# Neighbourhood attention: the value sums of two neighbouring units share one PSUM bank and are copied and added together

## The chip, the cores and the metric

One core of a Trainium2 chip. The kernel is one launch that computes a whole encoder layer for two sequences. The time is the device time of the launch in microseconds (us); three runs of the kernel before gave 2685.11, 2685.29 and 2685.42, median 2685.29. Engines: PE is TensorE's matmul row and PEld its weight loads, DVE is VectorE, ACT is ScalarE, POOL is GpSimd, SP is SyncE (it only issues DMAs).

## The reference

A layer runs two token mixers beside each other on the same input projection: 2-D neighbourhood attention and a bidirectional mLSTM. Both are gated, projected, merged and projected out. The change lies in the attention over the grid tokens (64 columns wide, 16 and 32 rows). Per row of queries and block of 16 columns it is:

```python
s_win = jnp.einsum('bcqhd,bwckhd->bhcqwk', q_blk, k_blk).astype(jnp.float32) * scale
s_win = jnp.where(valid[:, :, None, :], s_win + bias, NEG)
s_met = jnp.einsum('bcqhd,bmhd->bhcqm', q_blk, km).astype(jnp.float32) * scale
p = jax.nn.softmax(jnp.concatenate([s_met, s_win], axis=-1), axis=-1).astype(v.dtype)
return (jnp.einsum('bhcqm,bmhd->bcqhd', p_met, vm)
        + jnp.einsum('bhcqwk,bwckhd->bcqhd', p_win, v_blk))
```

A query sees 8 rows and 16 columns of keys around it and 16 learned meta tokens. The result is multiplied by silu(z) before the projection.

## The kernel before

All products run in single precision by splitting operands into a high and a low part (three matmuls, lines L218 to L220, for most dense products). TensorE's order is written by hand; the instructions of the other engines are ordered by a scheduler that simulates the program while it is built, and that also chooses which buffer of a pool a new tile gets.

The program has a sparse chain (mLSTM and attention, for the two sequences in turn) and a dense chain (input projections L787 to L789 and L988 to L990, final projections L1949 to L1951). A generator yields costs from the sparse chain, and dense matmuls are put between its steps until they have made up the cost. So in an attention stage TensorE always has dense matmuls between two steps of attention, and attention's other work runs on DVE and ACT meanwhile.

Attention walks over units. A unit is one tile of 8 query rows, one head of 64 channels and one block of 16 columns, 128 queries in all; the four blocks of a head follow each other. There are 64 units in the first stage and 128 in the second, 192 in all. A unit goes through a pipeline, spread over four to five rounds u of a loop with four steps each:

- round u: the scores (two matmuls L1236 and L1237, a "score group") go into a bank with the tag "sc" (one bank) for even units and "sm" (two banks) for odd ones; DVE adds the bias and finds the maximum (L1240); ACT takes the exponential (L1251, out of the bank to the tile prb)
- round u + 1: DVE divides by the sum (L1260, L1261)
- round u + 2: TensorE transposes the probabilities (L1268), ACT takes the high part (L1270) and DVE the low part (L1275)
- round u + 3, last step: three or four matmuls L1283 (a "value group") multiply by the values. The stationary operand holds the values' high part for output rows 0 to 63 and the low part for rows 64 to 127; the moving one holds the probabilities' high part in columns 0 to 127 and the low part in columns 128 to 255. So one "sm" bank gets four products in its first 256 columns, of which three are needed
- round u + 4: ACT copies one of them to the output tile yg (L1291, first step of the round), and DVE adds the two others in place (L1298, after the scaling in the round's second step), 64 partitions by 128 columns each. With the last block of a pair of heads yg is multiplied by the gate (L1300) and stored.

So an "sm" bank is taken three times in two rounds: by two value groups, which each keep it until their adds are done, and by one score group, which keeps it until its exponential is done.

Of the kernel before, what the change touches and what calls it, by code (L numbers as in the profile page):

```python
# [13 lines left out]
AF = mybir.ActivationFunctionType  # L14
ALU = mybir.AluOpType
# [3 lines left out]
P = 128  # L19
# [56 lines left out]
def _row_types(R):  # L76

    out = []
    for t in range(R // 8):
        if t == 0:  # L80
            out.append((0, 0, 11))
        elif t == R // 8 - 1:
            out.append((2, R - 12, 12))
        else:
            out.append((1, 8 * t - 4, 15))
    return out
# [52 lines left out]
class K:  # L139
# [964 lines left out]
    def na(self, s, rts):  # L1104

        tc, nc, i = self.tc, self.nc, self.i
        rows = _row_types(SEQLEN[s] // 64)
        with tc.tile_pool(name=f"na{s}{rts[0]}", bufs=1, side="right", reuse_waits="tile") as np_:
            self.qB = [np_.tile([P, 4, P], F32R, name=f"qB{j}") for j in range(2)]
            self.kx = [np_.tile([P, 16, 64], F32R, name=f"kx{j}") for j in range(2)]  # L1110
            self.gts = [np_.tile([P, 17, 48], F32, name=f"gt{j}") for j in range(2)]
            for q in self.qB:
                nc.gpsimd.dma_start(q[64:128], i["onehot"].rearrange("a (b c) -> a b c", b=4))
            for g in self.gts:
                nc.gpsimd.memset(g[:, 0, :], 0.0)
                nc.gpsimd.memset(g[:, 16, :], 0.0)
            heads = [(rt, pr, hh) for rt in rts for pr in range(4) for hh in range(2)]
            n = len(heads)
            prep = self.na_prep(np_, s, rows, heads, 0)
            self.na_bias(rows, heads, 0)  # L1120
            for k in range(6):
                next(prep, None)
                for _ in range(2 if k else 17 - 5 * s):
                    yield A_N[s]
            cur, nxt = self.head, None
            units = [(j, cb) for j in range(n) for cb in range(4)]
            ready = {}
            n_ = len(units)
            for u in range(n_ + 4):
                if u >= 4:  # L1130
                    self.na_copy(ready[u - 4])
                if u < n_:
                    j, cb = units[u]
                    if cb == 0:
                        cur = self.head
                        prep = self.na_prep(np_, s, rows, heads, j + 1) if j + 1 < n else iter(())
                        next(prep, None)
                    ready[u] = [cur, heads[j], cb, None, None, self.gts[j % 2], None]
                    self.na_scores(np_, ready[u], rows)
                    if j + 1 < n and cb == 0:  # L1140
                        self.na_bias(rows, heads, j + 1)
                yield A_N[s]
                if u < n_:
                    self.na_exp(np_, ready[u])
                if 1 <= u <= n_:
                    self.na_scale(np_, ready[u - 1])
                if u >= 4:
                    self.na_add(ready.pop(u - 4), s)
                if u < n_ and cb:
                    next(prep, None)  # L1150
                if u == n_ + 3:
                    break
                yield A_N[s]
                if 2 <= u <= n_ + 1:
                    self.na_turn(np_, ready[u - 2])
                    if u < n_ and cb >= 2:
                        next(prep, None)
                yield A_N[s]
                if 2 <= u <= n_ + 1:
                    self.na_low(ready[u - 2])  # L1160
                if u >= 3:
                    self.na_out(ready[u - 3])
                yield A_N[s]

    def na_bias(self, rows, heads, j):
# [108 lines left out]
        pts, pt, (_, _, nb, ks) = unit[4], unit[6], unit[3]  # L1274
        self.nc.vector.tensor_tensor(pts[:ks, :nb, 1, :], pt[:ks, :nb], pts[:ks, :nb, 0, :].bitcast(F32), op=ALU.subtract)  # L1275

    def na_out(self, unit):
        nc = self.nc
        vt, cb, (_, _, nb, ks), pts = unit[0][3], unit[2], unit[3], unit[4]
        kc = KC0[cb]  # L1280
        av = self.psum("sm", [P, 512])
        for ch in range(nb):
            nc.tensor.matmul(av[:, :256], vt[:ks, kc // 8 + ch].rearrange("p a b -> p (a b)"),  # L1283
                             pts[:ks, ch].rearrange("p a b -> p (a b)"), start=ch == 0, stop=ch == nb - 1)
        unit[6] = av

    def na_copy(self, unit):
        yg, cb, av, h0 = unit[0][4], unit[2], unit[6], unit[1][2] * 64
        yv = yg.rearrange("p (r b c) -> p b r c", r=8, b=4)[h0:h0 + 64, cb]
        rc = lambda x: x.rearrange("p (r c) -> p r c", r=8)  # L1290
        self.nc.scalar.activation(yv, rc(av[64:128, 0:P]), AF.Copy)  # L1291
        unit[4] = yv, rc

    def na_add(self, unit, s):
        nc = self.nc
        (_, _, _, _, yg, zt), (rt, pr, hh), cb, _, (yv, rc), _, av = unit
        for c in (0, P):
            nc.vector.tensor_tensor(yv, rc(av[0:64, c:c + P]), yv, op=ALU.add)  # L1298
        if hh and cb == 3:
            nc.vector.tensor_tensor(yg, yg, zt, op=ALU.mult)  # L1300
            nc.sync.dma_start(self.YA[s][rt][pr][:, :], yg)
            self.done.add(("na", s, rt, pr))
# [900 lines left out]
```

## Time and profile before

| | |
|---|---|
| median of 3 runs | 2685.29 us |
| profiled execution | 2684.88 us |
| its span, first to last instruction | 2682.8 us |
| mean granted TensorE clock | 0.996 |
| PE, PEld busy | 2640.1, 2330.7 us |
| DVE, ACT, POOL busy | 1940.1, 1441.0, 195.3 us |

The profile is of one execution. A row of a group of instructions gives the line, the engine, the operation, the tile written and the tiles read, the shapes and the count; behind the bar the busy time in us and the mean duration of one in ns; behind the second bar the idle time of the engine just before these instructions and what ended it. A row of the list of waits gives who waited for whom, the total in us, how many times, and the longest. A row of the timeline gives the start, the duration, the engine and the instruction, and in brackets how long the engine was idle before it. A row by stretches gives the stretch, its width, the busy time and count of PE, PEld, DVE, ACT and POOL, the granted clock, the share of the DMA engines and GB/s. A matmul's end is modelled, since matmuls overlap.

### The profile page before, as it was taken

The page shows a single profiled execution, that of the slowest core. Times are in us where ns is not written, and L with a number is a line of the kernel's source. Part 1 is how long each engine was busy: PE and PEld are TensorE (multiplying, and loading weights), DVE is VectorE, ACT ScalarE, POOL GpSimd, SP SyncE. Part 2 cuts the span into 40 slices and gives each one's busy share as a digit, 9 for nine tenths or more (in the row PEclk, how much of TensorE's full clock was granted, in tenths as well). Part 3 has the DMA queues.
Part 4 walks back from the last instruction along what each step waited for, and adds up shares of the span by engine and source line. Part 5 has one row for each costly group of instructions (what it writes and reads, how often), then busy time and mean ns, then how long its engine had stood idle before and what let it go on. Part 6 is the DMA issues. An engine that isn't in the chain of part 4 may idle for free.

```text
span 2682.8 us, 47074 instructions
## 1 busy us (share of the span) xinstructions
PE 2640.1 (98%) x15928; PEld 2330.7 (87%) x15928; DVE 1940.1 (72%) x5262; ACT 1441.0 (54%) x3388; POOL 195.3 (7%) x418
## 2 busy tenths in 40 slices
PE   9999998999999999999999999999999999999998
PEld 7998897899978999888888888887889898989888
DVE  5655678788667878546686776867478989898954
ACT  5423555554445655546665666656366666656521
POOL 0111130011301115000000000000000000000000
PEclk9999999999999999999999999999999999999999
DMA  9899988799866998978889998899899999998975
GB/s 370 331 334 335 331 289 306 278 339 312 294 223 235 328 331 289 319 234 285 261 270 346 362 299 261 273 351 336 281 312 319 288 306 287 280 304 261 310 255 209
DMA packets 393520, 800.49 MB, mean 298 GB/s; under 512 B 50528, under 2 KB 173360, under 8 KB 389440
## 3 DMA queue, kind: packets, MB, share of 16 engines
q1 hardware_dynamic: 361728, 697.24, 77.9%
q0 software_dynamic: 31552, 100.25, 10.1%
q8 instruction: 126, 2.06, 0.3%
q14 instruction: 114, 0.93, 0.1%
HBM read 543.72 MB, written 253.60 MB: 297 GB/s over the span
## 4 chain that ended last, share of the span: by engine, by line
PE 89%; DVE 4%; DMA 4%; ACT 1%; issue 1%; SPq 0%; POOL 0%; DVEq 0%; ACTq 0%
PE pj L218 9%; PE pj L220 9%; PE pj L219 9%; PE pj L988 8%; PE pj L990 7%; PE pj L989 7%; PE pj L787 5%; PE pj L789 5%; PE pj L788 5%; PE pj L1950 3%; PE pj L1949 3%; PE pj L1951 3%; PE sm L1283 3%; PE tr L1268 2%; DMA whl<-w 1%
## 5 line engine op out<-in xcount | busy, mean ns | idle before, releaser
L218 PE MATMUL pj<-xh,whl 128*128 128x512 f32 (+1 forms) x960 | 369.5, 385 | 8.2 <-DMA whl<-w 6.2
L220 PE MATMUL pj<-xh,whl 128*128 128x512 f32 (+1 forms) x960 | 361.3, 376 | 0.0
L219 PE MATMUL pj<-xl,whl 128*128 128x512 f32 (+1 forms) x960 | 360.4, 375 | 0.2 <-DVE xl L446 0.2
L787 PE MATMUL pj<-whl,xh 128*128 128x256 f32 (+1 forms) x1152 | 330.7, 287 | 0.0
L789 PE MATMUL pj<-whl,xl 128*128 128x256 f32 (+1 forms) x1152 | 327.0, 284 | 0.0
L788 PE MATMUL pj<-whl,xh 128*128 128x256 f32 (+1 forms) x1152 | 326.7, 284 | 0.0
L787 PEld LDWEIGHTS pj<-whl,xh 128*128 128x128 f32 x1152 | 219.0, 190 | 0.4
L1949 PE MATMUL pj<-whl,mh 128*128 128x256 f32 x768 | 218.3, 284 | 0.9 <-DMA whl<-w 0.9
L788 PEld LDWEIGHTS pj<-whl,xh 128*128 128x128 f32 x1152 | 218.9, 190 | 0.2
L789 PEld LDWEIGHTS pj<-whl,xl 128*128 128x128 f32 x1152 | 218.8, 190 | 0.0
L218 PEld LDWEIGHTS pj<-xh,whl 128*128 128x128 f32 x960 | 181.2, 189 | 40.8 <-issue 5.3
L1950 PE MATMUL pj<-whl,mh 128*128 128x256 f32 x768 | 216.3, 282 | 0.0
L1951 PE MATMUL pj<-whl,mlo 128*128 128x256 f32 x768 | 215.5, 281 | 0.0
L220 PEld LDWEIGHTS pj<-xh,whl 128*128 128x128 f32 x960 | 181.3, 189 | 35.0
L219 PEld LDWEIGHTS pj<-xl,whl 128*128 128x128 f32 x960 | 181.6, 189 | 30.4 <-issue 1.0
L988 PE MATMUL pj<-xh,whl 128*128 128x512 f32 x512 | 206.7, 404 | 1.1 <-ACT pj L1005 1.1
L990 PE MATMUL pj<-xh,whl 128*128 128x512 f32 x512 | 202.0, 395 | 0.0
L989 PE MATMUL pj<-xl,whl 128*128 128x512 f32 x512 | 201.0, 393 | 0.0
L1275 DVE TENSOR_TENSOR pts<-tr,pts 96x384 fp32r<-96x384 f32 (+2 forms) x192 | 118.6, 617 | 57.2 <-ACT pts L1270 55.2
L1270 ACT ACTIVATE pts<-tr 96x384 fp32r<-96x384 f32 (+2 forms) x192 | 103.6, 539 | 100.8 <-PE tr L1268 100.1
L218 PE MATMUL pj<-yh,whl 128*128 128x512 f32 x384 | 154.1, 401 | 0.0
L219 PE MATMUL pj<-yl,whl 128*128 128x512 f32 x384 | 151.5, 394 | 0.7 <-DVE yl L1851 0.7
(380 smaller groups left out, 6866.1 us busy)
## 6 DMA issues: line engine op xcount, KB each, us to landing
whl<-w SPq DMA_DIRECT2D x131, 1024.0 KB
whl<-q SPq DMA_DIRECT2D x112, 512.0 KB
w<-whl SPq DMA_DIRECT2D x36, 1024.0 KB
wraw<-wu SPq DMA_DIRECT2D x48, 512.0 KB
gt<-st SPq DMA_DIRECT2D x96, 256.0 KB
tg<-gt SPq DMA_DIRECT2D x96, 256.0 KB
q<-po POOLq DMA_DIRECT2D x26, 512.0 KB, 6.7
xt<-xt SPq DMA_DIRECT2D x24, 512.0 KB
```

Source lines behind the costliest of these rows:

```text
L218: mm(out, ah, bh, start=start, stop=False)
L219: mm(out, ah, bl, start=False, stop=False)
L220: mm(out, al, bh, start=False, stop=stop)
L787: nc.tensor.matmul(o, xh, wh, start=k == 0, stop=False)
L788: nc.tensor.matmul(o, xh, wl, start=False, stop=False)
L789: nc.tensor.matmul(o, xl, wh, start=False, stop=k == KT - 1)
L988: mm(bank, w[:, 0, k], xh[:, k], start=fresh and k == 0, stop=False, skip_group_check=True)
L989: mm(bank, w[:, 0, k], xl[:, k], start=False, stop=False, skip_group_check=True)
L990: mm(bank, w[:, 1, k], xh[:, k], start=False, stop=k == 3, skip_group_check=True)
L1949: nc.tensor.matmul(o, mh[:, k, xs], wh, start=clear > 0 and k == 0, stop=False)
L1950: nc.tensor.matmul(o, mh[:, k, xs], wl, start=False, stop=False)
L1951: nc.tensor.matmul(o, ml[:, k, xs], wh, start=False, stop=clear < 2 and k == KT - 1)
```

## The change

A bank "sm" is taken for two neighbouring units. The value group of the even unit writes columns 0 to 255 and that of the odd unit, one round later, columns 256 to 511. When the odd one is done, one copy and two adds handle both units: they work on 64 partitions by 2 x 128 columns. They stand where the odd unit's stood: the copy in the first step of the next round, the adds in its second step (behind the last unit, directly after the copy). Copies go from 192 to 96 and adds from 384 to 192. Matmuls keep their number, their shapes and their order.

```diff
             for u in range(n_ + 4):
-                if u >= 4:
-                    self.na_copy(ready[u - 4])
+                if u >= 5 and u % 2:
+                    self.na_copy(ready[u - 5], pairs[u - 5])
+                    if u > n_:
+                        self.na_add(ready[u - 5], pairs.pop(u - 5), s)
...
-                if u >= 4:
-                    self.na_add(ready.pop(u - 4), s)
+                if 5 <= u <= n_ and u % 2:
+                    self.na_add(ready[u - 5], pairs.pop(u - 5), s)
...
                 if u >= 3:
-                    self.na_out(ready[u - 3])
+                    if u % 2:
+                        pairs[u - 3] = self.psum("sm", [P, 512])
+                    self.na_out(ready[u - 3], pairs[(u - 3) // 2 * 2])
...
-    def na_out(self, unit):
+    def na_out(self, unit, av):
...
-        av = self.psum("sm", [P, 512])
+        o = av[:, cb % 2 * 256:cb % 2 * 256 + 256]
         for ch in range(nb):
-            nc.tensor.matmul(av[:, :256], vt[:ks, kc // 8 + ch].rearrange("p a b -> p (a b)"),
+            nc.tensor.matmul(o, vt[:ks, kc // 8 + ch].rearrange("p a b -> p (a b)"),
...
+    def na_copy(self, unit, av):
+        h0 = unit[1][2] * 64
+        yv = unit[0][4].rearrange("p (r b c) -> p b r c", r=8, b=4)[h0:h0 + 64, unit[2]:unit[2] + 2]
+        rc = lambda x: x.rearrange("p (b q r c) -> p b q r c", b=2, q=2, r=8)
+        self.nc.scalar.activation(yv, rc(av[64:128])[:, :, 0], AF.Copy)
...
-        for c in (0, P):
-            nc.vector.tensor_tensor(yv, rc(av[0:64, c:c + P]), yv, op=ALU.add)
-        if hh and cb == 3:
+        for q in range(2):
+            nc.vector.tensor_tensor(yv, rc(av[0:64])[:, :, q], yv, op=ALU.add)
+        if hh and cb == 2:
```

Lines behind the change stand 5 lower in the changed file up to the value group (score group L1241 and L1242, transposes L1273, value group L1288), the copy is L1295, the adds are L1302 and the gate L1304.

What a group of matmuls on an "sm" bank waits for, counted in the two built programs by the last instruction of DVE and ACT that its first matmul names:

| | before | changed |
|---|---|---|
| score groups on "sm" | 96: 92 an add, 4 nothing of DVE or ACT | 96: 3 an add, 5 an exponential, 88 nothing of DVE or ACT |
| value groups that take a bank | 192: 58 an add, 42 an exponential, 92 only their own low part | 96: 42 an add, 50 an exponential, 4 only their own low part |
| value groups on the second half | none | 96: only their own low part |

TensorE at the place of the program that runs at 889 to 893 us in the profile before. The dense matmuls are those on "pj"; the names in brackets are the semaphores that an instruction waits for, DVE_49 that of VectorE, Activation_49 that of ScalarE, PE_49 TensorE's own, DMAHW those of DMAs. Before:

```order
L218 MATMUL pj<-xh,whl 128x512
L219 MATMUL pj<-xl,whl 128x512
L220 MATMUL pj<-xh,whl 128x512
L1283 MATMUL sm<-pts,vt 128x256 [waits DVE_49]
L1283 MATMUL sm<-pts,vt 128x256 x2
L1236 MATMUL sm<-kd,stk 128x288 [waits DVE_49,Activation_49]
```

And changed:

```order
L218 MATMUL pj<-xh,whl 128x512
L219 MATMUL pj<-xl,whl 128x512
L220 MATMUL pj<-xh,whl 128x512
L1288 MATMUL sm<-pts,vt 128x256 [waits DVE_49]
L1288 MATMUL sm<-pts,vt 128x256 x2
L1241 MATMUL sm<-kd,stk 128x288 [waits PE_49]
```

No matmul has moved; the score group no longer names VectorE and ScalarE.

VectorE at the same place. "xr" is a tile of other work (it prepares weights for later), "yg" is written by the adds, L1240 and L1245 are the bias and maximum. Before:

```order
L641 TENSOR_TENSOR xr<-xh,xl 128x1024 x2
L1298 TENSOR_TENSOR yg<-sm,yg 64x8x16
L1260 RECIPROCAL sm<-sm 128x1
L1275 TENSOR_TENSOR pts<-tr,pts 96x3x128
L1212 TENSOR_TENSOR kx_9711<-kx_9711,kd 64x768
L1298 TENSOR_TENSOR yg<-sm,yg 64x8x16
L1261 TENSOR_SCALAR prb<-prb,sm 128x384
L705 SCALAR_TENSOR_TENSOR st<-st 128x512
L1298 TENSOR_TENSOR yg<-sm,yg 64x8x16
L1240 ISA sm,mx<-sm,gt_9712 128x288
```

And changed:

```order
L641 TENSOR_TENSOR xr<-xh,xl 128x1024 x2
L1265 RECIPROCAL sm<-sm 128x1
L1280 TENSOR_TENSOR pts<-tr,pts 96x3x128
L1217 TENSOR_TENSOR kx_9711<-kx_9711,kd 64x768
L1266 TENSOR_SCALAR prb<-prb,sm 128x384
L1245 ISA sm,mx<-sm,gt_9712 128x288
L1245 ISA mx 128x1
L705 SCALAR_TENSOR_TENSOR st<-st 128x512
L641 TENSOR_TENSOR xr<-xr 128x512
L1302 TENSOR_TENSOR yg<-sm,yg 64x2x8x16
```

The two adds of the even unit, which stood ahead of the score's maximum, are gone; the pair's first add stands behind it. Elsewhere the scheduler has also moved rows that the change does not touch: in 210 places on DVE, 88 on ACT, 12 on POOL and 56 on SP, nearly all of them by a few rows.

More of the change, by code (lines that the diff above doesn't have):

```diff
@@ L1128, in na @@
             n_ = len(units)
+            pairs = {}
             for u in range(n_ + 4):
-                if u >= 4:
-                    self.na_copy(ready[u - 4])
+                if u >= 5 and u % 2:
+                    self.na_copy(ready[u - 5], pairs[u - 5])
+                    if u > n_:
+                        self.na_add(ready[u - 5], pairs.pop(u - 5), s)
                 if u < n_:
@@ L1280, in na_out, with na_add @@
         kc = KC0[cb]
-        av = self.psum("sm", [P, 512])
+        o = av[:, cb % 2 * 256:cb % 2 * 256 + 256]
         for ch in range(nb):
-            nc.tensor.matmul(av[:, :256], vt[:ks, kc // 8 + ch].rearrange("p a b -> p (a b)"),
+            nc.tensor.matmul(o, vt[:ks, kc // 8 + ch].rearrange("p a b -> p (a b)"),
                              pts[:ks, ch].rearrange("p a b -> p (a b)"), start=ch == 0, stop=ch == nb - 1)
[L1285 to L1291, printed above, removed]
+    def na_copy(self, unit, av):
[3 more added lines that the diff above has]
+        self.nc.scalar.activation(yv, rc(av[64:128])[:, :, 0], AF.Copy)
         unit[4] = yv, rc
-    def na_add(self, unit, s):
+    def na_add(self, unit, av, s):
         nc = self.nc
-        (_, _, _, _, yg, zt), (rt, pr, hh), cb, _, (yv, rc), _, av = unit
-        for c in (0, P):
-            nc.vector.tensor_tensor(yv, rc(av[0:64, c:c + P]), yv, op=ALU.add)
-        if hh and cb == 3:
+        (_, _, _, _, yg, zt), (rt, pr, hh), cb, _, (yv, rc) = unit[:5]
+        for q in range(2):
+            nc.vector.tensor_tensor(yv, rc(av[0:64])[:, :, q], yv, op=ALU.add)
+        if hh and cb == 2:
             nc.vector.tensor_tensor(yg, yg, zt, op=ALU.mult)
```

## The prediction

> **What bounds the kernel now.** I read the page's totals and its chain first, then the two stages in which the changed code runs (their first and last instructions of lines L1291 and L1298 lie at 851.8 and 2575.6 us), then the waits of TensorE, and last the place of the longest wait. The totals and the chain:
>
> ```profile
> span 2682.8 us, 47074 instructions
> ...
> PE 2640.1 (98%) x15928; PEld 2330.7 (87%) x15928; DVE 1940.1 (72%) x5262; ACT 1441.0 (54%) x3388; POOL 195.3 (7%) x418
> ...
> PE 89%; DVE 4%; DMA 4%; ACT 1%; issue 1%; SPq 0%; POOL 0%; DVEq 0%; ACTq 0%
> ```
>
> TensorE's matmul row (PE) is busy for 2640.1 of 2682.8 us and makes up 89% of the chain. VectorE (DVE) and ScalarE (ACT), on which the change removes work, have 28% and 46% to spare. So what the change does to the time is what it does to TensorE's waits. The two attention stages, from the table by stretches (width, then busy time of each engine, granted clock, DMA share, GB/s):
>
> ```profile
> 853.00:1072.00 219.00, 215.61 (x1645) 208.38 (x1644) 178.02 (x426) 123.40 (x253) 60.96 (x109) 0.99 0.89 304
> 1987.00:2577.00 590.00, 585.20 (x3898) 533.37 (x3899) 514.87 (x1299) 354.10 (x854) 2.31 (x4) 1.00 0.93 293
> ```
>
> PE is idle there for 3.4 + 4.8 = 8.2 us in all. TensorE's list of waits says for whom (total us, times, longest):
>
> ```profile
> PE pj L218 <- DMA whl<-w: 6.2, 2, 3.9
> PE sm L1236 <- DVE yg L1298: 4.3, 5, 1.9
> ...
> PE sm L1283 <- ACT prb L1251: 2.0, 3, 1.3
> ...
> PE sm L1236 <- DVE sm L1260: 1.5, 2, 0.9
> ...
> PE sm L1283 <- DVE yg L1298: 0.2, 1, 0.2
> ```
>
> The last four are all that attention's own matmuls wait for, and all are waits for one of the two "sm" banks: the score group L1236 for 4.3 + 1.5 us, the value group L1283 for 2.0 + 0.2. (L1260 is the instruction that ended nearest; the score group itself names only an add and a copy.) The longest of them in order of time:
>
> ```profile
> 889.60 0.52 PE L1283 MATMUL sm<-pts,vt 96*128 96x256 f32 x3
> ...
> 889.78 0.28 DVE L1298 TENSOR_TENSOR yg<-sm,yg 64x128 f32<-64x128 f32 x1
> ...
> 890.10 0.16 DVE L1260 RECIPROCAL sm<-sm 128x1 f32<-128x1 f32 x1
> 890.18 0.53 DVE L1275 TENSOR_TENSOR pts<-tr,pts 96x384 fp32r<-96x384 f32 x1
> ...
> 890.63 0.94 DVE L1212 TENSOR_TENSOR kx<-kx,kd 64x768 fp32r<-64x768 f32 x1
> ...
> 891.60 0.28 DVE L1298 TENSOR_TENSOR yg<-sm,yg 64x128 f32<-64x128 f32 x1
> ...
> 892.03 0.37 PE L1236 MATMUL sm<-kd,stk 128*128 128x288 f32 x1 [1.91 <-DVE yg L1298]
> ...
> 892.37 0.28 PE L787 MATMUL pj<-whl,xh 128*128 128x264 f32 x1
> ...
> 892.49 0.28 PE L788 MATMUL pj<-whl,xh 128*128 128x264 f32 x1
> ...
> 893.14 0.42 PE L789 MATMUL pj<-whl,xl 128*128 128x264 f32 x1
> ...
> 893.36 0.42 PE L787 MATMUL pj<-whl,xh 128*128 128x264 f32 x1
> ```
>
> The two adds of one unit do not follow each other on VectorE: three other operations stand between them, the second ends at 891.88, and only then may the score group write. Two things are read off beside it. Matmuls in a row start 0.12 us apart and last 0.28, so a wait costs its idle time and 0.16 more. And from 893.14 on they start 0.22 apart. The table by stretches of 3.4 us around it:
>
> ```profile
> 889.35:892.76 3.41, 1.50 (x11) 1.25 (x10) 3.28 (x8) 3.31 (x6) 0.00 (x0) 1.00 1.04 396
> 892.76:896.18 3.42, 3.42 (x18) 3.42 (x17) 3.27 (x10) 0.59 (x2) 0.00 (x0) 0.50 1.05 393
> 896.18:899.60 3.42, 3.42 (x31) 3.42 (x30) 3.05 (x7) 0.87 (x2) 0.00 (x0) 1.00 0.99 342
> ```
>
> After a stretch in which PE worked for 1.50 of 3.41 us the granted clock is 0.50 for 3.42 us, with 18 matmuls instead of 31.
>
> **The change part by part.** *Removed work.* The rows by line, of the changed operations and of two that move 256 columns from a bank as the new ones do:
>
> ```profile
> L1298 DVE TENSOR_TENSOR yg<-sm,yg 64x128 f32<-64x128 f32 x384 | 107.7, 281 | 27.6 <-ACT yg L1291 20.6
> ...
> L1291 ACT ACTIVATE yg<-sm 64x128 f32<-64x128 f32 x192 | 52.6, 274 | 67.0 <-PE sm L1283 63.5
> L1956 DVE TENSOR_TENSOR yo<-pj,gain 128x256 f32<-128x256 f32 x96 | 40.4, 421 | 42.4 <-ACT sqj L1955 41.8
> L1955 ACT ACTIVATE sqj<-pj 128x256 bf16<-128x256 f32 x96 | 36.6, 381 | 64.3 <-PE pj L1951 56.1 <-DVE yo L1956 7.6
> ```
>
> 384 adds of 281 ns (107.7 us) become 192, which I price at the 421 ns of L1956: 80.8 us, 26.9 less on VectorE. 192 copies of 274 ns (52.6 us) become 96 at the 381 ns of L1955: 36.6 us, 16.0 less on ScalarE. Both lie beside TensorE's work, which covers them: 0 on the path. If that cover went, at most the 42.9 us would count.
>
> *Score groups.* (The counts here and below are of waits in the two built programs, given with the change.) Of the 96 that use an "sm" bank, 92 name an add before; 3 do in the changed program, and 5 an exponential of two rounds ago. Of the 7 waits that go, the cost is 4.3 + 1.5 + 7 x 0.16 = 6.9 us. I take -6.9; nothing is late next for them, since a matmul of the same stream stands ahead.
>
> *Clock.* If the 1.91 us at 892.03 go, PE has no hole there, and the stretch of half clock with it. At 0.22 instead of 0.12 us a matmul, 3.42 us did the work of 1.87: -1.6 (-1.7 by the clock's 0.50, -1.4 by 18 matmuls against 31).
>
> *Value groups, exponential.* A pair's bank is taken in every second round, and which of the two it is was settled by the scheduler. 42 of 192 value groups name the exponential before and 50 of 96 now. Their price today is 2.0 + 3 x 0.16 = 2.5 us; by 50/42 it becomes 3.0: +0.5.
>
> *Value groups, adds.* 58 of 192 name an add before, at 0.2 + 0.16 = 0.4 us in all; now 42 do, the other first groups of pairs. For each the copy and adds end later: 0.38 + 2 x 0.42 against 0.27 + 2 x 0.28, 0.39 us more. This wait is not in the trace. Its low bound is the present rate of value groups, 42/58 x 0.4, a change of -0.1. Its high bound is the rate of the score groups, 6.9/92 a piece: 42 x 0.075 = 3.2, a change of +2.8. I take +1.8, two thirds up, because the chain is longer and TensorE is not asked for less in between. Behind such a wait stands all of TensorE: the next dense matmuls.
>
> *Order of the rest.* Rows of DVE, ACT, SP and POOL that the change does not touch stand in a few hundred other places from about 893 us on; TensorE's do not. I price it at 0. A weight load that comes late is the row to bound it with: 3.9 + 0.16, so +4.1; a wait of that kind that goes is worth about as much the other way in principle, but attention has none.
>
> Sum: -6.9 - 1.6 + 0.5 + 1.8 = -6.2 us. The profiled execution took 2684.88 us (the span and 2.1 around it), so 2678.7; the median of the runs is 0.4 above it, so 2679.1, 0.23% less.
>
> **Rivals.** *The wait moves over (no change).* The pair's first group takes up all that the score groups leave: 6.9 for the adds in place of 1.8, -6.9 - 1.6 + 0.5 + 6.9, about 2684.2. For it: the same adds on the same crowded VectorE, 0.39 us later, and value groups that already wait for an exponential. Against it: the value group comes three quarters of a round behind the score group, and in 58 cases such a group waited once.
>
> *The clock stretch stays (no change).* Then the sum lacks 1.6: 2680.7. For it: only one stretch is concerned, and a hole of another origin can bring it back. Against it: the table's three rows. [...]
>
> *A late weight load (no change).* The order of SP's queue moves in 56 places, among them four loads "whl<-w". One late by 4.1 us gives 2683.2. Against it: in attention no such wait stands in the list.
>
> *The freed engines reach the end (faster).* If the shorter queues of VectorE and ScalarE also clear the value groups' waits, all of them go: -6.9 - 1.6 - 2.5 - 0.4 = -11.4, 2673.9. [...]
>
> *The longer hold is in the way (slower).* A pair's bank is held for two rounds and freed 0.39 us later. Where TensorE reaches the next pair before that, each of 96 pairs costs 0.39. To be 0.2% slower, the 8.5 us gained, less 0.5, and 5.4 more have to be eaten: 13.4 / 0.39 = 34 pairs. With 40 of them 2692.8. For it: VectorE is busy 178.0 of 219.0 us in the first stage and 514.9 of 590.0 in the second. Against it: 7 waits in 92 score groups, which come sooner after the adds.
>
> **How the numbers follow.** 0.2% is 5.4 us, about what a measurement of this kernel can tell from no change: 2679.9 and 2690.7 are the bounds. The forecast has 0.42 and is faster; the engines freed 0.09, faster; the wait that moves 0.20, the clock 0.10, the late load 0.08, all within; the longer hold 0.11, slower. That makes 0.51 faster, 0.38 within and 0.11 slower. The forecast alone spans 2677.2 to 2680.1 by the bounds of its adds. The range for 8 in 10 goes from the 2673.9 of the freed engines to 2687, where the late load is added to a wait that has moved over (2684.2 + 4.1, less part of the clock) and the longer hold begins.
>
> **What would show it.** Right: no idle of PE at the score groups for an add, a list in which value groups wait for the adds by 1 to 3 us and for the exponential by about 3, a clock of 1.00 at 893 to 896 us, 192 adds near 421 ns and 96 copies near 381. Wrong: adds or copies much longer than that; waits of the value groups near 9 us; a wait for "whl" in attention; a new stretch of half clock.

## The result, and the profile after

The changed kernel took 2677.35 us (median of 7 runs, 2675.68 to 2681.7); the kernel before, run beside it, 2685.11 (7 runs, 2681.5 to 2686.68). The ratio is 0.9977 with a 95% interval of 0.9967 to 0.9986, so it is faster by 0.23%. In a second session it was 2679.09 against 2684.69, ratio 0.9979 (0.9970 to 0.9988). One of that session's 11 runs of the changed kernel took 4314.22 us at a granted clock of 0.556, as one of the third session's 15 of the kernel before took 3208.49 at 0.751; the ratios leave both out. The forecast of 2679.1 equals the second of the two medians, and both medians are inside the likeliest case's own range (2677.2 to 2680.1). The total was right; two of its terms and a term set to zero were off, and partly cancelled.

The totals and the chain of the changed kernel's page:

```profile
span 2673.9 us, 46686 instructions
...
PE 2637.4 (99%) x15928; PEld 2329.0 (87%) x15928; DVE 1916.3 (72%) x5070; ACT 1424.9 (53%) x3292; POOL 195.7 (7%) x418
...
PE 87%; DMA 7%; DVE 4%; ACT 2%; issue 1%; SPq 0%; DVEq 0%; ACTq 0%
```

The span is 8.9 us shorter, while DVE is busy 23.8 us less and ACT 16.1 less: the saved work did not come off the time one for one. The rows by line of what was merged, and of the two groups that share the "sm" banks:

```profile
L1288 PE MATMUL sm<-pts,vt 96*128 96x256 f32 (+2 forms) x672 | 116.1, 289 | 5.0 <-ACT prb L1256 4.1 <-DVE yg L1302 0.7
...
L1302 DVE TENSOR_TENSOR yg<-sm,yg 64x256 f32<-64x256 f32 x192 | 79.6, 414 | 15.5 <-ACT yg L1295 12.1
...
L1295 ACT ACTIVATE yg<-sm 64x256 f32<-64x256 f32 x96 | 36.6, 381 | 31.9 <-PE sm L1288 26.3 <-DMA zt<-nz 1.3 <-DMA kx<-nk 1.3
...
L1241 PE MATMUL sm<-kd,stk 128*128 128x384 f32 (+2 forms) x96 | 32.6, 340 | 0.0
```

An add of both units takes 414 ns and a copy 381, against the 421 and 381 that the forecast took from L1956 and L1955. The score groups on "sm" (L1241 now) have no idle time left. Of TensorE's list of waits, the rows that answer to those of before:

```profile
PE sm L1288 <- ACT prb L1256: 4.1, 6, 1.4
PE pj L218 <- DMA whl<-w: 3.4, 1, 3.4
...
PE sm L1347 <- issue: 2.0, 1, 2.0
...
PE sm L1288 <- DVE yg L1302: 0.7, 1, 0.7
```

The value groups' wait for an exponential has doubled (2.0 to 4.1). At L1347, a gate matmul of the second mLSTM stage, there is a wait that was 0.5 us before (L1343); "issue" means that the profile found nothing that released it.

To see where the time went I cut the program at the same four matmuls in every kernel: the first score group of attention's stage one, the last matmul of its last value group, the first score group of stage two, and the last value group's last matmul. All kernels here issue the same 15928 matmuls in the same order, so the stretches can be compared. Between the cuts, the table by stretches of the kernel before (width, busy time of PE, PEld, DVE, ACT and POOL, clock, DMA share, GB/s; rows: stage one, middle, stage two):

```profile
833.93:1196.71 362.78, 359.11 (x2365) 328.26 (x2363) 257.87 (x629) 197.44 (x410) 63.84 (x124) 1.00 0.88 295
1196.71:1936.16 739.45, 734.80 (x3655) 611.44 (x3654) 509.35 (x1702) 441.55 (x1162) 4.11 (x22) 1.00 0.91 301
1936.16:2573.26 637.10, 632.10 (x4122) 571.82 (x4121) 543.60 (x1374) 385.81 (x924) 2.31 (x4) 1.00 0.93 294
```

And of the changed kernel:

```profile
828.40:1185.29 356.89, 356.61 (x2365) 326.46 (x2364) 249.12 (x565) 191.53 (x378) 64.22 (x124) 1.00 0.87 300
1185.29:1927.21 741.92, 735.50 (x3655) 611.42 (x3654) 509.15 (x1702) 442.33 (x1162) 4.10 (x22) 1.00 0.90 300
1927.21:2564.32 637.11, 632.15 (x4122) 572.30 (x4121) 528.28 (x1246) 374.06 (x860) 2.18 (x4) 1.00 0.93 294
```

Stage one is 5.9 us shorter: PE's idle time there went from 3.7 us (362.78 - 359.11) to 0.3, and PE's busy time fell by the 2.5 that matmuls at half clock (1.5, at 892 us) and behind waits had taken. Stage two is as long as before, with 5.0 us idle in both. The middle, which the change does not touch, is 2.5 us longer. The rest of the span's difference, 5.5 us, lies ahead of attention (833.93 against 828.40), where every engine issues the same instructions in the same order in both programs: over the 13 profiles of this study that first part took between 828.4 and 836.4 us. TensorE's waits there for a late weight load (L218 for "whl<-w") are 6.2 us in the profile before and 3.4 in this one; half clock lasts for 10.2 us there in both. So of the 8.9 us between these two profiles 5.5 are put down to chance, and 3.4 belong to attention and the middle (4.6 between the second profiles of the two kernels). The medians, with the scatter of the first part in them, say 7.8 and 5.6; the 1 to 4 us by which they are larger are found in no stretch here.

### The profile page after: what moved, and what is told of

Same layout as the page of the kernel before. It is cut to its first block, busy times and chain, and to the rows that moved or that the text cites. A ratio compares the mean times of both kernels' runs of the same rounds, so it can differ in the third digit from the quotient of the medians.

```text
span 2673.9 us, 46686 instructions
## 1 busy us (share of the span) xinstructions
PE 2637.4 (99%) x15928; PEld 2329.0 (87%) x15928; DVE 1916.3 (72%) x5070; ACT 1424.9 (53%) x3292; POOL 195.7 (7%) x418
## 4 chain that ended last, share of the span: by engine, by line
PE 87%; DMA 7%; DVE 4%; ACT 2%; issue 1%; SPq 0%; DVEq 0%; ACTq 0%
PE pj L218 9%; PE pj L220 9%; PE pj L219 9%; PE pj L988 8%; PE pj L990 7%; PE pj L989 7%; PE pj L787 5%; PE pj L789 5%; PE pj L788 5%; PE pj L1954 3%; PE pj L1953 3%; PE pj L1955 3%; PE sm L1288 2%; PE tr L1273 2%; DMA wraw<-wu 2%; DMA whl<-w 1%
## 5 line engine op out<-in xcount | busy, mean ns | idle before, releaser
L218 PE MATMUL pj<-xh,whl 128*128 128x512 f32 (+1 forms) x960 | 369.8, 385 | 5.0 <-DMA whl<-w 3.4
L1955 PE MATMUL pj<-whl,mlo 128*128 128x256 f32 x768 | 215.4, 280 | 0.0
L218 PEld LDWEIGHTS pj<-xh,whl 128*128 128x128 f32 x960 | 181.4, 189 | 37.1 <-issue 4.8
L1275 ACT ACTIVATE pts<-tr 96x384 fp32r<-96x384 f32 (+2 forms) x192 | 103.5, 539 | 102.6 <-PE tr L1273 101.8
L218 PE MATMUL pj<-yh,whl 128*128 128x512 f32 x384 | 154.1, 401 | 0.0
```

The lines of the kernel that those rows point to most:

```text
L218: mm(out, ah, bh, start=start, stop=False)
L1955: nc.tensor.matmul(o, ml[:, k, xs], wh, start=False, stop=clear < 2 and k == KT - 1)
```

## The experiments

Two theories were tried. **Banks**: the gain comes from the score groups' waits for an "sm" bank, which end because the bank is asked for two times in two rounds and no longer three; the saved operations are worth nothing. **Work**: the gain comes from the shorter queues of VectorE and ScalarE. Medians are in us. Stages are those of the cuts above, one profiled execution each:

| kernel | median (runs) | ratio to before (95%) | stage one | middle | stage two |
|---|---|---|---|---|---|
| before | 2685.11 (7) | | 362.78 | 739.45 | 637.10 |
| before, second profile | 2687.07 (1) | | 362.72 | 739.17 | 637.40 |
| changed | 2677.35 (7) | 0.9977 (0.9967 to 0.9986) | 356.89 | 741.92 | 637.11 |
| changed, second time | 2679.09 (11) | 0.9979 (0.9970 to 0.9988) | 356.86 | 741.76 | 636.03 |
| pair, small operations | 2684.26 (10) | 1.0000 (0.9991 to 1.0009) | 357.01 | 746.18 | 638.18 |
| the same, loads held in order | 2681.35 (10) | 0.9990 (0.9978 to 1.0002) | 357.05 | 740.35 | 637.16 |
| before, all scores on "sc" | 2678.32 (10) | 0.9978 (0.9969 to 0.9987) | 356.88 | 739.53 | 636.53 |
| changed, all scores on "sc" | 2677.63 (7) | 0.9970 (0.9958 to 0.9981) | 356.85 | 742.05 | 633.68 |
| changed, loads held in order | 2678.31 (10) | 0.9976 (0.9966 to 0.9985) | 356.85 | 739.94 | 634.82 |
| before, three banks | 2672.40 (4) | 0.9954 (0.9938 to 0.9970) | 356.86 | 739.07 | 631.41 |
| before, three banks, again | 2672.66 (4) | 0.9959 (0.9942 to 0.9975) | 356.86 | 738.93 | 632.95 |
| changed, three banks | 2672.17 (4) | 0.9954 (0.9939 to 0.9969) | 356.86 | 741.33 | 628.99 |
| changed, three banks, loads held | 2671.35 (5) | 0.9950 (0.9937 to 0.9962) | 356.85 | 740.41 | 629.41 |

The kernel before, run beside them, had medians of 2685.11, 2684.69, 2685.74 and 2684.81 in the four sessions; each ratio is to the runs of its own session. Single runs of one kernel lie up to 12 us apart (2672.64 to 2684.52 for "before, all scores on sc"), so the end of one profile says little, and a difference of 2 us between two of these medians is not resolved.

**The two kernels a second time.** No edit. What was expected of the changed kernel:

> The changed kernel once more. Two theories of the 8.9 us between the two profiled spans. Banks: about 6 us of it arise in the attention stages (score groups' waits and a stretch of half clock gone, value groups' waits 3 us longer), and the 5.3 us that the changed kernel is ahead at the start of attention are chance of that execution. Then this execution has again no wait of a score group, about 5 us of waits of value groups (4.1 for the exponential, 0.7 for the adds the first time), and it need not be ahead at the start of attention: there it lies anywhere from 0 to 6 us earlier than the kernel before; the ratio over the rounds stays at 0.9965 to 0.9985. Whole: the 5.3 us belong to the change as well; then they appear again, and the ratio goes to 0.9967 or lower.

And of the kernel before:

> The kernel before once more, for a second profile. Both theories: the attention stages show the same waits for the adds at the score groups (5.8 us) within 1 us; the stretch ahead of attention, where the first profile of the changed kernel was 5.3 us ahead, differs from the first profile by up to some us, by DMA and clock alone.

The stages come back within 0.3 us in the kernel before, and within 0.2 us in the changed one but for stage two (1.1). In the kernel before the wait of the score groups for an add is 4.3 us in 5 waits again. In the changed one the value groups wait 3.4 us for the exponential and 0.2 for adds.

**The pair without the saved operations.** The pair shares its bank and is handled in the same round as in the changed kernel, but with two copies and four adds of 128 columns for it, so that 192 and 384 remain. Against the changed kernel:

```diff
-        self.nc.scalar.activation(yv, rc(av[64:128])[:, :, 0], AF.Copy)
+        for b in range(2):
+            self.nc.scalar.activation(yv[:, b], rc(av[64:128])[:, b, 0], AF.Copy)
...
-        for q in range(2):
-            nc.vector.tensor_tensor(yv, rc(av[0:64])[:, :, q], yv, op=ALU.add)
+        for b in range(2):
+            for q in range(2):
+                nc.vector.tensor_tensor(yv[:, b], rc(av[0:64])[:, b, q], yv[:, b], op=ALU.add)
```

> The pair still shares a bank, but each unit is copied and added by operations of its own, in the round in which the pair was: 192 copies and 384 adds as before the change. Banks: score groups do not come back to waiting for adds in most places (20 of 96 name an add in the built program, 92 before the change), but the chain behind a pair is longer still (2 copies and 4 adds, 0.55 + 1.12 us against 0.38 + 0.83), so value groups wait longer, 6 to 10 us; time 0 to 5 us above the changed kernel, at or under the kernel before. Work: the gain came from the 27 us less on VectorE and 16 us less on ScalarE; it is lost, and the time is that of the kernel before (2685) or above.

Its median is that of the kernel before, so by the median alone "work" would have won. The stages say otherwise: stage one has the whole gain, 357.01. It was lost elsewhere, 6.7 us in the middle and 1.1 in stage two. Its list of waits:

```profile
PE sm L1288 <- ACT prb L1256: 5.4, 9, 1.3
PE sm L1349 <- issue: 4.0, 1, 4.0
```

The wait of 4.0 us is at the gate matmul of the second mLSTM stage (L1349 here), the place where the changed kernel waits for 2.0. What stands behind it was followed below ("loads held in order").

**The kernel before, all scores on "sc".** No pair, no operation saved; score groups no longer take an "sm" bank:

```diff
-        sc = self.psum("sc" if self.turns else "sm", [P, 512])
+        sc = self.psum("sc", [P, 512])
```

> The kernel before, with one edit: all score groups use the one bank of the tag sc, so that the two sm banks are left to the value groups and no value group shares a bank with a neighbour. No operation is saved. Banks: score groups no longer wait for adds, value groups have two rounds for them and wait for nothing but their own low part; the score groups instead wait for the exponential of the round before, 0 to 6 us in all. The gain of the change comes back without any saved operation, or most of it: 2676 to 2682. Work: nothing is gained, since VectorE and ScalarE do the same work: 2684 to 2687.

One line that saves no instruction gives the gain of the whole change: 0.9978, and stage one 356.88. In stage two the score groups now wait for the exponential that reads their one bank:

```profile
PE sc L1236 <- ACT prb L1251: 3.9, 4, 2.5
```

**The changed kernel, all scores on "sc".** The same line in the changed kernel.

> The changed kernel with all score groups on the one bank of the tag sc. Banks: the value groups' waits for the exponential and the adds (4.1 + 0.7 us in the profile after) go, the score groups wait for the exponential of the round before instead; net gain of 0 to 4 us against the changed kernel, 2673 to 2679. Work: the same time as the changed kernel, 2677.

The median, 2677.63, fits both theories as they were put. Stage two is 2.9 us shorter than in the kernel with the same banks and the unmerged operations (633.68 against 636.53), of which some 1.5 (an estimate, the price of the stretch at 892 us) is a stretch of half clock that the latter has beside its wait of 2.5 us (from 2150 to 2160 us PE is busy for 7.53 us, at a clock of 0.83). The middle is 2.5 us longer and takes it back. The medians of these two kernels, 0.7 us apart, cannot be told apart.

**Loads held in order.** In the changed kernel SyncE issues one weight load of the dense chain ahead of the loads of the second mLSTM stage, where before it stood behind them. SyncE's rows of the timeline in the kernel before:

```profile
1202.08 0.41 SPq L1316 DMA_DIRECT2D g_t<-gg  x1
1202.53 0.42 SPq L1317 DMA_DIRECT2D g_t<-gg  x1
1203.81 1.60 SPq L304 DMA_DIRECT2D whl<-q3s  x1
```

And in the changed kernel:

```profile
1189.75 0.32 SPq L304 DMA_DIRECT2D whl<-q3s  x1
1190.12 0.43 SPq L1461 DMA_DIRECT2D tri<-tri  x1
...
1193.06 0.41 SPq L1320 DMA_DIRECT2D g_t<-gg  x1
1193.51 0.42 SPq L1321 DMA_DIRECT2D g_t<-gg  x1
```

"whl<-q3s" may go out only when TensorE has freed its buffer (SyncE's issues of L304 waited for that in the changed kernel for 3.1 us in two waits, the longer one 1.7), and the gate loads "g_t<-gg" stood behind it. The gate matmuls need what DVE and ACT make of "g_t". Their own row before:

```profile
1212.73 0.63 PE L1343 MATMUL sm<-g_lf,tri 128*128 128x68 f32 x4 [0.49 <-PE pj L990]
```

And in the changed kernel:

```profile
1202.36 0.30 DVE L1341 TENSOR_TENSOR g_lf<-g_lf,g_e 128x136 f32<-128x136 f32 x1
1202.76 0.63 PE L1347 MATMUL sm<-g_lf,tri 128*128 128x68 f32 x4 [1.95 <-issue]
```

The matmul starts 0.10 us behind the end of VectorE's last operation on its operand "g_lf". Without its idle time the matmul would have come 1202.76 - 1.95 - 1193.06 = 7.75 us behind the first gate load, against 1212.73 - 0.49 - 1202.08 = 10.16 us before: the load lost 2.4 us on TensorE, and 1.95 of it became a wait. The edit has the next such weight load issued behind the gate loads (line numbers rise by 4 to 6):

```diff
+                with ExitStack() as st:
+                    if self.pin is not None:
+                        st.enter_context(self.tc.issue_after(self.pin))
+                    self.pin = None
+                    for x, k in zip((hi, lo), key[1:]):
+                        nc.sync.dma_start(x[:, :n].bitcast(F32), self.qd[k][:, :])
...
+        if s:
+            self.pin = next(x for x in reversed(nc.cur_bb.bb.instructions) if x.engine == mybir.EngineType.SP)
```

> The changed kernel with one dependency more: the next weight load of the dense chain (whl<-q) is issued behind the two gate loads (g_t<-gg) at the start of the second mLSTM, as in the kernel before. Reorder: the wait of L1347 (2.0, 1.5, 1.5 and 4.0 us in the four paired profiles, 0.5 and 0.2 without pairs) comes from that load, which stands ahead of the gate loads on SP in the changed kernel; with the edit it is 0.5 us or less, no stretch of half clock lies between 1200 and 1216 us, and the time falls by 1.5 to 3 us, to 2674.5 to 2677. Chance: the wait is one of DMA luck and stays at 1.5 to 2 us; 2677 to 2679.

The place did what was wanted. The gate loads stand ahead of the weight load again, and the gate matmul waits 0.48 us as before:

```profile
1194.37 0.41 SPq L1324 DMA_DIRECT2D g_t<-gg  x1
1194.82 0.42 SPq L1325 DMA_DIRECT2D g_t<-gg  x1
1195.35 1.64 SPq L308 DMA_DIRECT2D whl<-q3s  x1
...
1204.69 0.63 PE L1353 MATMUL sm<-g_lf,tri 128*128 128x68 f32 x4 [0.48 <-PE pj L994]
```

The middle fell from 741.92 to 739.94: matched matmul by matmul, the 3.0 us that the changed kernel lost at the gate matmul are gone, and smaller steps elsewhere took 1.0 back. The median did not follow: 2678.31, between the two of the changed kernel and in the range of "chance". A gain of 2 us is too small for this spread, so what the load costs is shown by the place and not by the time. Then the same edit in the pair with small operations, where it was worth most:

> The pair shares a bank but keeps 192 copies and 384 adds of 128 columns, and in the second mLSTM stage the next load "whl<-q" is issued behind the two gate loads. Theory 'banks and load order': the saved operations are worth nothing, and what the kernel without the pin lost against the changed one was lost in the middle, behind the gate loads. Then the middle falls from 746.2 to about 740 us, the wait of the gate matmul goes, stage one stays at 356.9, and the median is 2677 to 2680. Theory 'work': the small operations cost VectorE and ScalarE time on the path; the middle stays at 743 or more or stage two rises above 638, and the median stays at 2683 or more.

Here the middle fell from 746.18 to 740.35, as the first theory said, and the wait at the gate matmul from 4.0 to 0.7 us. The median, 2681.35, fell between the bounds of both theories, 1.4 above those of the first. What is left against the changed kernel with the same edit is stage two, 637.16 against 634.82, and the waits there are for the exponential, 5.1 us in 8 against 2.8 in 5. The interval of its ratio reaches past 1 (1.0002), so by the medians this kernel is not told from the kernel before. The small operations seem to cost something, though not in stage one.

**Three banks under one tag.** If banks are what is short, the single "sc" bank and the two "sm" banks serve both groups better as one pool of three. Nothing else changes:

```diff
-BANKS = dict(pj=3, tr=2, sc=1, sm=2)
+BANKS = dict(pj=3, tr=2, sm=3)
...
-        sc = self.psum("sc" if self.turns else "sm", [P, 512])
+        sc = self.psum("sm", [P, 512])
```

(Other users of "sc" take "sm" as well.) Of the kernel before it was expected:

> The kernel before with the tags sc and sm made one tag with three banks, from which each score group and each value group takes the bank that comes free first; no pairs, all 192 copies and 384 adds. Banks: it is the number of times that a bank is taken in two rounds, against the banks there are, that counts: four takings of three banks against three takings of two; waits of attention fall from 8 us to 1 to 4, and the time to 2676 to 2681. Work: 2684 to 2687.

And of a second measurement:

> The kernel before with three banks a second time. Banks: 2670 to 2674 us, stage two 630.5 to 632.5, middle 739 to 740. If the first measurement was luck, 2676 or more.

It beats both kernels: 0.9954 and 0.9959, twice the gain of the change, with every one of the 384 adds. The first median, 2672.40, lies 3.6 us below the range that "banks" had for it; stage two of the second profile, 632.95, is 0.45 above its range. Of the waits in stage two one row is left in the first of the profiles:

```profile
PE sm L1283 <- DVE pts L1275: 0.9, 1, 0.9
```

Its stage two has 1.2 us of PE idle where there were 5.0:

```profile
1928.90:2560.31 631.41, 630.17 (x4123) 572.54 (x4121) 541.17 (x1374) 384.99 (x924) 2.04 (x4) 1.00 0.93 296
```

In the second profile two waits of the score groups for adds came back, 1.1 us in all, with three of 0.2 to 0.3 us beside them. The pair on top of three banks, without and with the loads held:

> The changed kernel with one tag of three banks for scores and sums, without the pin. Theory 'banks': the waits for "sm" in attention are gone as in the kernel before with three banks, stage one 356.9 and stage two 629 to 632 us; the middle stays at about 742 as in the changed kernel. Median 2671 to 2674. If the pair were of use beside three banks, stage two would be 2 us below that of the kernel before with three banks (631.4); if not, within 1 us of it.

> The changed kernel with the three banks of one tag and the weight load behind the gate loads. Banks and reorder: attention's waits fall to 0 to 1.5 us and the wait of L1347 to 0.5; 4 to 7 us under the changed kernel, 2671 to 2675. Work: as the changed kernel, 2677.

```profile
1928.86:2557.85 628.99, 628.99 (x4122) 572.43 (x4121) 526.40 (x1246) 374.29 (x860) 2.05 (x4) 1.00 0.94 299
```

The row is stage two without the held loads. PE has no idle time left there, and the stage is 2.4 to 4.0 us shorter than with three banks alone. The time hardly shows it: 2672.17 against 2672.40 and 2672.66. Against three banks alone the middle is 2.3 us longer without the held loads and 1.3 with them, and at the very end of the program a weight load came late in both of these profiles:

```profile
PE pj L1953 <- DMA whl<-w: 2.1, 1, 2.1
```

(2.7 us with the loads held; 0.9 and 1.0 in the kernel before). Behind the wait of 2.1 us matmuls start 0.21 us apart from 2643.97 to 2647.17 us, and 0.12 apart around that. The part from the last cut to the last matmul took 104.4 and 105.0 us in place of 101.7 to 101.9. The fastest kernel measured is the changed one with three banks and held loads, 2671.35 us, 0.50% faster than the kernel before; its lead over the other kernels with three banks lies within their intervals.

## Why the prediction was right, point by point

The attention stages together gave what the forecast's sum has, -5.9 us in the first profile and -7.0 in the second against -6.2. That the medians agree with it so well is in part luck: the middle took 2.3 to 2.9 us back, and the medians hold 1 to 4 us of gain that no stretch accounts for.

**Score groups, -6.9: right, -7.8.** Matched matmul by matmul, eight steps of this kind are gone in the profiled run, at 892, 992, 1047, 1069, 1987, 2152, 2280 and 2379 us of the kernel before: 2.14 + 1.12 + 0.72 + 0.35 + 0.92 + 0.85 + 0.70 + 1.04 = 7.84 us. The one at 1069 is not in the list of waits. That the banks are the cause, and not the freed engines, is shown by the kernel with the scores on "sc", which keeps all operations.

**Clock, -1.6: right, -1.5 by the same matching.** The wait at 892 us and the half clock behind it stood in both profiles of the kernel before (matmuls 0.22 us apart in the first; a clock of 0.59 from 894.20 to 897.60 us in the second), whose stage one is 362.78 and 362.72 us; in the other eleven it is 356.85 to 357.05. At the same place of the program the changed kernel shows:

```profile
886.41:889.83 3.42, 3.42 (x31) 3.42 (x30) 3.36 (x8) 2.11 (x5) 0.00 (x0) 1.00 1.05 383
```

31 matmuls and a clock of 1.00, where there were 18 and 0.50. The rival that the stretch stays is out. How many executions of the kernel before have this stretch is open: two of two profiles show it.

**Value groups, exponential, +0.5: mis-sized.** They cost 4.1 + 6 x 0.16 = 5.1 us (4.4 in the second profile) in place of 2.5: +2.6 and +1.9. The term scaled the old price by the number of groups that name an exponential. But the price is set by how late the exponential ends, and that moved. At the three largest new waits (2020, 2080 and 2130 us in the first profile), counted from the matmul 40 places ahead, TensorE is there as early as before, and the exponential ends 1.3, 2.0 and 2.1 us later. The last of them, before:

```profile
2132.81 0.69 DVE L1240 CUSTOM_DVE_ANT_1 sm<-sm,gt 128x512 f32<-128x512 f32 x1
...
2133.42 0.42 DVE L1261 TENSOR_SCALAR prb<-prb,sm 128x384 f32<-128x384 f32 x1
2133.60 0.69 ACT L1251 ACTIVATE prb<-sm,mx 128x512 f32<-128x512 f32 x1 [1.65 <-DVE mx L1240]
2133.75 0.69 DVE L1918 TENSOR_TENSOR mlo<-tg,mh 128x512 fp32r<-128x512 f32 x1
...
2134.35 0.75 DVE L2046 SCALAR_TENSOR_TENSOR yo<-yo,nwy,xres 128x512 f32<-128x512 f32 x1
...
2134.97 0.60 PE L1283 MATMUL sm<-pts,vt 128*128 128x256 f32 x3
```

And in the changed kernel:

```profile
2126.16 0.42 DVE L1266 TENSOR_SCALAR prb<-prb,sm 128x384 f32<-128x384 f32 x1
2126.49 0.69 DVE L1922 TENSOR_TENSOR mlo<-tg,mh 128x512 fp32r<-128x512 f32 x1
2127.09 0.75 DVE L2050 SCALAR_TENSOR_TENSOR yo<-yo,nwy,xres 128x512 f32<-128x512 f32 x1
2127.76 0.70 DVE L1245 CUSTOM_DVE_ANT_1 sm<-sm,gt 128x512 f32<-128x512 f32 x1
...
2129.01 0.49 ACT L1275 ACTIVATE pts<-tr 128x384 fp32r<-128x384 f32 x1 [3.26 <-PE tr L1273]
2129.39 0.68 ACT L1256 ACTIVATE prb<-sm,mx 128x512 f32<-128x512 f32 x1
...
2130.22 0.50 PE L1288 MATMUL sm<-pts,vt 128*128 128x256 f32 x2 [1.31 <-ACT prb L1256]
```

The scheduler put VectorE's bias and maximum (L1240, now L1245) behind three rows that it stood ahead of before, and the exponential needs its result. On ScalarE the exponential stands behind the high part of another unit (L1275), which waited for TensorE's transposes. So here it is the moved order of the two engines' rows, which the prediction set to 0, that costs. Two smaller waits (2278 and 2376 us) are of the kind of the rival "the wait moves over": TensorE, no longer held up by a score group, comes 0.7 and 1.0 us earlier and the exponential 0.5 and 0.8, which costs 0.2 us each. With three banks these waits are gone from the list, so it is again the bank that the exponential holds.

**Value groups, adds, +1.8: mis-sized.** 0.7 + 0.16 = 0.9 us in the first profile and 0.4 in the second, against 0.4 before: +0.5 and 0. The rate of the value groups, which the text gave as the low bound, was the better one; the choice of two thirds up was not borne out. The rival of the longer hold, 0.39 us for each of 34 pairs or more, found one pair.

Together the two terms measured +3.1 and +1.9 where the forecast had +2.3. So the forecast's sum for waits of attention held, but by two errors of opposite sign, which is luck.

**Order of the rest, 0: wrong, about +2.5 us.** The middle grew by 2.3 to 2.9 us (741.92 and 741.76 against 739.45 and 739.17). The prediction named four "whl<-w" loads that move on SP, and looked for a late weight load in attention. The load that mattered is another, "whl<-q3s", and what came late was a load behind it, in another stage. Matched matmul by matmul, the gate matmul lost 3.0 us in the first profile, half clock behind it included, and 1.0 in the second. The rest of the middle's difference comes from small steps and from the half clock at 1817.77 us of the kernel before: it lasts for 3.41 us there and is missing in the first profile of the changed kernel (-1.5; the clock is 1.00 from 1800 to 1830 us). In the second profile PE is busy in the middle for 0.8 us more than in the first (736.31 against 735.50).

**Freed DVE and ACT work, 0: not quite.** In stage one it is worth nothing: 356.9 with and 357.0 without. In stage two, the merged operations go with 2.9 us less (scores on "sc", some 1.5 of it the half clock), 2.0 to 4.0 (three banks), 2.3 (pairs with held loads) and 1.1 to 2.2 (pairs without), one profile for most, and the same kernel's stage two differs by up to 1.5 between two profiles. So some 2 us is likely; the exact size stays open, and so does whether the saved work does it or the order in which the scheduler put each program's rows. It is far from the 44 us of adds and copies that were saved (107.7 - 79.6 and 52.6 - 36.6), and of the change's own stage two it shows nothing, since the exponential's waits stand in for the ones removed.

**The rivals' faster end**, 2673.9 with all of attention's waits gone, was not reached by the change. The kernel with three banks and pairs reached it: its stage two has no idle time at all, and it took 2672.17 us.

**The signs.** No score group waits for an add, the clock is 1.00 at the place, and adds and copies took 414 and 381 ns, as named. The value groups' waits for adds (0.7 and 0.2 us) are under the 1 to 3 named, those for the exponential (4.1 and 3.4) above the 3. Of the signs that it gave for being wrong one appeared: a new stretch of half clock, at the gate matmul.

## What to carry to other kernels

When TensorE waits for a bank, count how often a bank of that pool is taken per round and by whom, before counting the work of the engines that empty it: here one pool of three banks gave twice what halving the operations gave. Price a wait by when the operation that ends it will be done in the new schedule, and not by how many groups name it: here the same exponential ended up to 2.1 us later because rows of VectorE and ScalarE had moved. And when a scheduler reorders a DMA queue, look for what stands behind each load that moved, in all stages. Where runs spread by more than the effect, compare the same stretch of the program between fixed instructions, not the ends.

## What the runs showed that was not expected

In the changed kernel half clock came anew behind the 1.95 us at the gate matmul:

```profile
1200.61:1204.02 3.41, 1.46 (x9) 1.15 (x9) 3.23 (x9) 2.29 (x4) 0.00 (x0) 1.00 0.97 356
1204.02:1207.43 3.41, 3.41 (x11) 2.56 (x10) 1.48 (x6) 1.46 (x4) 0.00 (x0) 0.50 1.03 330
1207.43:1210.84 3.41, 3.41 (x19) 2.42 (x18) 1.89 (x10) 1.37 (x4) 0.00 (x0) 0.99 0.64 225
```

PE worked for 1.46 of 3.41 us and then got 0.50 for 3.41 us, nearly the figures at 892 us before (1.50 of 3.41, with a wait of 1.91). In the second profile of the changed kernel the same wait was 1.47 us, and the clock stayed at 1.00 (1203.50 to 1210.30 us).

The length of the wait alone did not decide it here. In the first profile of the changed kernel a later wait of 2.65 us (L1703, which starts at 1809.29) was followed by no half clock:

```profile
1804.79:1808.21 3.42, 1.84 (x8) 1.13 (x6) 0.33 (x2) 0.69 (x1) 0.00 (x0) 1.00 1.08 374
1808.21:1811.62 3.41, 1.98 (x9) 1.58 (x10) 1.38 (x4) 2.36 (x7) 0.00 (x0) 1.00 0.65 195
1811.62:1815.03 3.41, 3.41 (x20) 2.97 (x19) 2.89 (x9) 2.16 (x7) 0.00 (x0) 1.00 0.95 330
```

PE worked for 1.84 and 1.98 us in the first two of these stretches, and the clock was 1.00 in all three. What sets this wait apart from those of 1.91 and 1.95 us was not shown.

Stretches of half clock also stand ahead of attention, at other times in each of these two profiles: in the kernel before at 691.38 us for 6.83 us and at 793.78 for 3.41, in the changed kernel at 439.47 for 6.83 and at 787.63 for 3.41.
